# Operand sums of the FFN output placed between the products of the FFN input, in a ring of their own

## The chip, the cores and the metric

The kernel runs on one core of a Trainium2 chip. The core has five engines with queues of their own: TensorE (PE) multiplies matrices, VectorE (DVE) and ScalarE (ACT) work element by element, GpSimd (POOL) does the same and cannot read PSUM, and SyncE (SP) issues DMA transfers. Each engine runs its instructions in the order of its queue and waits at the first one that is not ready. The metric is the device time of one execution in microseconds.

## What is computed

One layer of a hybrid decoder on 1024 tokens of width 1024, in float32: token mixing, cross attention and a gated FFN. The change touches the last part:

```python
def conv_glu(hn, w_ffn_in, conv_w, conv_b, w_ffn_out):
    S = hn.shape[1]
    a, gate = jnp.split(hn @ w_ffn_in, 2, axis=-1)
    a_pad = jnp.pad(a, ((0, 0), (CONV_W - 1, 0), (0, 0)))
    conv = conv_b + sum(a_pad[:, j:j + S] * conv_w[j] for j in range(CONV_W))
    return (jax.nn.gelu(conv) * gate) @ w_ffn_out
```

`w_ffn_in` is 1024 x 5632 and `w_ffn_out` 2816 x 1024.

## The kernel before

Every float32 operand of a product is split into a high and a low part, and one product of tiles is three matmuls: high by high, high by low, low by high (`mm3`, L280 to L283). The two FFN products also use Strassen's scheme in Winograd's form: seven products of half the size take the place of eight, at the price of sums of operands before and of results after.

**FFN input.** The 2816 columns are worked in FT = 22 steps f of 128 columns of `a` and 128 of `gate`. For each f, `Weights` loads two raw tiles of 512 KB (L162), A with the columns of `a` and B with those of `gate`; the ring of raw tiles has two slots (`NRAW`). Four jobs turn them into seven pages of split weights (ring of 12, `NWP`). Job A splits two pieces of the first tile. Job B makes three sums on GpSimd (L199, L200, L201) and splits two pieces. Job C makes one more sum on GpSimd (L207) and splits two. Job D splits the last piece. Splitting is a cast on ScalarE (L175) and a subtraction on VectorE (L178), in `parts`. The raw slots come free with the last L178 of jobs C and D. In a steady f, the calls of `W.pump` do jobs C and D for f + 1, then A and B for f + 2.

`ffn_in(f)` issues the seven products (`product`, 12 matmuls each) and combines the results on VectorE (`add`, L1421) with three temporaries `p1`, `u2`, `v5`. Then come the convolution and GELU (L1458 on ScalarE, L1459 and L1460 on VectorE, L1461 on ScalarE), the product with the gate (L1462 on VectorE), and the store of 128 rows of the result to `u_d` in DRAM (L1463).

**FFN output.** Its Winograd operands are sums of blocks, four for each pair of f on the side of `u_d` and four on the side of `w_ffn_out`. They are made during the FFN input by `fo_sums(side, m)` and kept in DRAM (`us_d`, `ws_d`). A call loads four tiles of 256 KB (L1502), does four sums on GpSimd (L1505) and four stores from GpSimd's queue (L1521). The call stands at the end of an f: for the weights (`"w"`) at odd f, for the activations (`"u"`) at even f. A sum of `u` needs two rows of blocks that were stored by two f before.

The temporaries `p1`, `u2`, `v5`, the four tiles of each call and the residual tiles `hr` of the FFN output share one ring of nine 2 KB slots per partition (`w2`, L1153).

**Who sets the order.** From f = 1 on no engine's order is written by hand. The program goes to a planner (`schedule_with_timeline_sim=True`), which walks a simulated timeline and gives each engine the earliest instruction of the program that is ready there. The order of the source is a priority, then, and an instruction can run well before its place in the source when its operands and its slot are there. On the chip each engine keeps the order that the planner wrote down.

Of the kernel before, what the change touches and what calls it, by code (L numbers as in the profile page):

```python
# [9 lines left out]
F32 = mybir.dt.float32  # L10
# [4 lines left out]
OP = mybir.AluOpType  # L15
# [3 lines left out]
P = 128  # L19
# [25 lines left out]
def hybrid_layer(ctx, tc, I, out):  # L45
    nc = tc.nc
    pe, act, dve, pool, sp = nc.tensor, nc.scalar, nc.vector, nc.gpsimd, nc.sync

    def open_pool(name, **kw):
        st = ExitStack()  # L50
        p = st.enter_context(tc.tile_pool(name=name, bufs=1, reuse_waits="tile", **kw))
        return st, p
# [8 lines left out]
    def nm(s):  # L61
        cnt[0] += 1
        return f"{s}_{cnt[0]}"
# [216 lines left out]
    def mm3(o, lh, ll, rh, rl, start, stop):  # L280
        pe.matmul(o, lhsT=lh, rhs=rh, start=start, stop=False)  # L281
        pe.matmul(o, lhsT=lh, rhs=rl, start=False, stop=False)  # L282
        pe.matmul(o, lhsT=ll, rhs=rh, start=False, stop=stop)  # L283
# [10 lines left out]
    def kq(shape, dt, name):  # L294
        return wpool.tile(shape, dt, name=nm(name), tag="kq", bufs=4)
# [630 lines left out]
    for s in range(-4, NB):  # L926
        h, i = b_units[max(s, 0)]
        m = s % NT
# [137 lines left out]
    for s in range(-2, NA + 3):  # L1066
# [21 lines left out]
        u = s - 2  # L1088
# [59 lines left out]
    pgp = ctx.enter_context(tc.tile_pool(name="pgp", bufs=1, reuse_waits="tile"))  # L1148

    def page(shape, dt, name):  # L1150
        return pgp.tile(shape, dt, name=nm(name), tag="pg", bufs=28)

    def w2(shape, dt, name):  # L1153
        return pgp.tile(shape, dt, name=nm(name), tag="w2", bufs=9)

    def page_s():
        return pgp.tile([P, 512], F32, name=nm("ws"), tag="ws", bufs=1)
# [97 lines left out]
    def xo_unit(c, t, mid=None):  # L1255
        pages = W.get(("xo", c), 8)
        half, u = divmod(t, 4)
        p = accp()
        for k in range(KT):
            oh, ol = ox[k // 4, (k % 4) // 2, half]  # L1260
            s = slice(u * P, (u + 1) * P)
            if k == 4 and mid:
                mid()
            mm3(p, oh[:, k % 2, s], ol[:, k % 2, s], pages[k][:, 0, :], pages[k][:, 1, :], k == 0, k == KT - 1)
        hs = h2[t][:, c * 512:(c + 1) * 512]
        dve.tensor_tensor(hs, p, hs, op=OP.add)
        if t == NT - 1:
            W.free(8)
        W.pump(1)

    def f_norm(t):
        rs = slice(t * P, (t + 1) * P)
        act.dma_start(h2_d[rs, :], h2[t])
        st = small("st", (P, 12), 6)
        ws = [w2([P, 512], F32, "hn") for _ in range(1 if t >= 4 else 2)]
        norm_rows(h2[t], ws[0].bitcast(BF), st[:, 0:1], st[:, 1:2])
        hn = []
        for g in range(2):
            hg = h2[t][:, g * 512:(g + 1) * 512]
            w = hg if t >= 4 else ws[g]  # L1280
            dve.scalar_tensor_tensor(w, hg, st[:, 1:2], gff[g], op0=OP.mult, op1=OP.mult)
            hn.append(w)
        hst[t] = hn
# [31 lines left out]
    def xb_finish(name):  # L1315

        if name == "T4":
            xb_new(name)
            for u in range(4):
                xb_put(name, u, t4s[u], "a", "d")  # L1320
            return
        XB[name] = [[], []]
        for v in range(2):
            f = tf[name][v]
            hh, ll = (page([P, 2, 512], F32R, name) for _ in range(2))
            act.copy(hh, f)
            dve.tensor_tensor(ll, f, hh.bitcast(F32), op=OP.subtract)
            XB[name][0].append(hh)
            XB[name][1].append(ll)
# [75 lines left out]
    def product(w, xb):  # L1405
        o = (PB[nprod[0]] if nprod[0] < len(PB) else (accp, trp, big)[nprod[0] % 3])()[:, 0:512]
        nprod[0] += 1
        for k in range(4):
            ks = slice(k * P, (k + 1) * P)
            hh, hl = (XB[xb][i][k // 2][:, k % 2, :] for i in range(2))  # L1410
            mm3(o, w[:, 0, ks], w[:, 1, ks], hh, hl, k == 0, k == 3)
        W.free(1)
        return o

    def ffn_in(f):

        def wt(n):
            return W.get(("fi", f), n + 1)[n]

        def add(o, x, y):  # L1420
            dve.tensor_tensor(o, x, y, op=OP.add)  # L1421
        a, g = kq([P, T], F32, "fa"), kq([P, T], F32, "fg")
        lo, hi = slice(0, 512), slice(512, 1024)
        p1 = w2([P, 512], F32, "p1")
        P1 = product(wt(0), "B11")
        act.copy(p1, P1)
        if f == 0:
            yield
            add(a[:, lo], product(wt(1), "B21"), p1)
            yield  # L1430
            P3 = product(wt(5), "B22")
            yield
        u2, v5 = (w2([P, 512], F32, n) for n in ("u2", "v5"))
        add(u2, product(wt(2), "T2"), p1)
        W.pump(1)
        if f:
            add(a[:, lo], product(wt(1), "B21"), p1)
            W.pump(1)
        add(v5, product(wt(3), "T1"), u2)
        W.pump(1)  # L1440
        P7 = product(wt(4), "T3")
        add(g[:, hi], P7, v5)
        add(u2, P7, u2)
        W.pump(1)
        if f:
            P3 = product(wt(5), "B22")
        if f == FT - 1:
            for n in range(FLD):
                fo_load(n)
        add(a[:, hi], P3, v5)  # L1450
        add(g[:, lo], product(wt(6), "T4"), u2)
        W.pump(1)
        if f == FT - 1:
            for n in range(2):
                fo_prep(n)
            nprep[0] = 2
        cv = kq([P, T], F32, "fc")
        act.activation(cv, a, AF.Identity, bias=cw[:, f, 3:4], scale=cw[:, f, 2:3])  # L1458
        dve.scalar_tensor_tensor(cv[:, 1:], a[:, :T - 1], cw[:, f, 1:2], cv[:, 1:], op0=OP.mult, op1=OP.add)  # L1459
        dve.scalar_tensor_tensor(cv[:, 2:], a[:, :T - 2], cw[:, f, 0:1], cv[:, 2:], op0=OP.mult, op1=OP.add)  # L1460
        act.activation(cv, cv, AF.Gelu_apprx_tanh)  # L1461
        dve.tensor_tensor(g, cv, g, op=OP.mult)  # L1462
        act.dma_start(u_d[f * P:(f + 1) * P, :], g)  # L1463
        if f % 2:
            fo_sums("w", f // 2)
        elif f:
            fo_sums("u", f // 2 - 1)
        if f == FT - 1:
            fo_sums("u", f // 2)

# [19 lines left out]
    def sum_at(d, j, m):  # L1492
        return d[(j * NM + m) * P:(j * NM + m + 1) * P, :]

    def fo_sums(side, m):

        src, d = (u_src, us_d) if side == "u" else (w_src, ws_d)
        x = {}
        for odd in range(2):
            for half in range(2):  # L1500
                x[odd, half] = w2([P, 512], F32, "fs")
                sp.dma_start(x[odd, half], src(m, odd, half))  # L1502

        def sub(o, p, q, op=OP.subtract):
            pool.tensor_tensor(o, p, q, op=op)  # L1505
        if side == "u":
            a11, a12, a21, a22 = x[0, 0], x[1, 0], x[0, 1], x[1, 1]
            sub(a22, a21, a22, OP.add)
            sub(a21, a11, a21)
            sub(a11, a22, a11)  # L1510
            sub(a12, a12, a11)
            made = (a22, a11, a21, a12)
        else:
            b11, b21, b12, b22 = x[0, 0], x[1, 0], x[0, 1], x[1, 1]
            sub(b11, b12, b11)
            sub(b12, b22, b12)
            sub(b22, b22, b11)
            sub(b21, b21, b22)
            made = (b11, b22, b12, b21)
        for j, y in enumerate(made):  # L1520
            pool.dma_start(sum_at(d, j, m), y)  # L1521

    FO_X = {"1": lambda m: u_src(m, 0, 0), "2": lambda m: u_src(m, 1, 0), "4": lambda m: u_src(m, 1, 1),
            "5": lambda m: sum_at(us_d, 0, m), "6": lambda m: sum_at(us_d, 1, m), "7": lambda m: sum_at(us_d, 2, m),
# [5 lines left out]
    def fo_load(n):  # L1530
        if n >= len(fo_steps):
            return
        i, m = fo_steps[n]
        fo_raw[n] = page([P, 2, 512], F32, "fo")
        sp.dma_start(fo_raw[n][:, 0, :], FO_X[i](m))
        sp.dma_start(fo_raw[n][:, 1, :], FO_Y[i](m))

    def fo_prep(n):

        if n >= len(fo_steps):  # L1540
            return
        raw = fo_raw.pop(n)
        hi, lo = wp(), wp()
        act.copy(hi, raw)  # L1544
        dve.tensor_tensor(lo, raw, hi.bitcast(F32), op=OP.subtract)  # L1545
        fo_pg[n] = (hi, lo)

    with tc.manual_schedule(engines={mybir.EngineType.PE}):
        for t in range(NT):
            xo_unit(1, t, (lambda: f_tr(t - 2)) if t >= 2 else None)  # L1550
            f_norm(t)
        first = ffn_in(0)
        next(first)
        f_tr(6)
        next(first)
        f_tr(7)
        next(first)
        for n in ("T1", "T2", "T3", "T4"):
            xb_finish(n)
        for _ in first:  # L1560
            pass
    for f in range(1, FT):
        for _ in ffn_in(f):
            pass
# [112 lines left out]
```

## Time and profile before

| | us |
|---|---|
| median of 3 runs | 1742.68 |
| lowest and highest run | 1738.83, 1744.15 |
| profiled execution | 1739.45 |
| its span, first to last instruction | 1737.7 |
| mean granted clock of TensorE, share of full speed | 0.969 |

The rows further down come from the profiled execution. Their times count from the start of its span.

### The profile page before, as it was taken

The page shows a single profiled execution, that of the slowest core. Times are in us where ns is not written, and L with a number is a line of the kernel's source. Part 1 is how long each engine was busy: PE and PEld are TensorE (multiplying, and loading weights), DVE is VectorE, ACT ScalarE, POOL GpSimd, SP SyncE. Part 2 cuts the span into 40 slices and gives each one's busy share as a digit, 9 for nine tenths or more (in the row PEclk, how much of TensorE's full clock was granted, in tenths as well). Part 3 has the DMA queues.
Part 4 walks back from the last instruction along what each step waited for, and adds up shares of the span by engine and source line. Part 5 has one row for each costly group of instructions (what it writes and reads, how often), then busy time and mean ns, then how long its engine had stood idle before and what let it go on. Part 6 is the DMA issues. An engine that isn't in the chain of part 4 may idle for free. (4 is left out here: it accounts for less than half of the span.)

```text
span 1737.7 us, 22708 instructions
## 1 busy us (share of the span) xinstructions
PE 1585.9 (91%) x7660; PEld 1292.1 (74%) x7660; DVE 1255.5 (72%) x2461; ACT 737.3 (42%) x1469; POOL 676.5 (39%) x862
## 2 busy tenths in 40 slices
PE   8999898778888999989999979989898888989998
PEld 7788676667777779878777857767676666768887
DVE  5746998999999895367452798777666677745564
ACT  6545577566664236135431343332322232343432
POOL 2647567455320230231010065556655555541111
PEclk9999999899989999999999989999999999999999
DMA  8221134222131211342030223544444454799611
GB/s 281 88 85 57 63 103 158 70 92 75 53 98 39 95 61 49 127 158 85 25 110 12 86 73 134 177 147 152 154 157 164 163 170 166 258 356 391 239 43 49
DMA packets 117796, 220.08 MB, mean 127 GB/s; under 512 B 18480, under 2 KB 38448, under 8 KB 117680
## 3 DMA queue, kind: packets, MB, share of 16 engines
q1 hardware_dynamic: 103744, 171.44, 29.8%
q0 software_dynamic: 8320, 27.27, 4.1%
q10 hardware_dynamic: 5616, 19.93, 3.0%
q8 instruction: 60, 0.98, 0.2%
q14 instruction: 56, 0.46, 0.1%
HBM read 160.92 MB, written 57.67 MB: 126 GB/s over the span
## 5 line engine op out<-in xcount | busy, mean ns | idle before, releaser
L178 DVE TENSOR_TENSOR wp<-raw,wp 128x512 fp32r<-128x512 f32 (+1 forms) x200 | 166.8, 846 | 125.0 <-ACT wp L175 116.8
L175 ACT CAST wp<-raw 128x512 fp32r<-128x512 f32 (+1 forms) x188 | 111.4, 615 | 233.4 <-POOL raw L201 123.1
L1545 DVE TENSOR_TENSOR wp<-fo,wp 128x1024 fp32r<-128x1024 f32 x77 | 102.2, 1345 | 83.0 <-ACT wp L1544 64.6
L1505 POOL TENSOR_TENSOR fs<-fs,fs 128x512 f32<-128x512 f32 x88 | 128.7, 1462 | 40.1 <-DMA fs<-u_d 28.9
L1544 ACT CAST wp<-fo 128x1024 fp32r<-128x1024 f32 x77 | 79.5, 1049 | 118.5 <-PE trp L283 43.5
L281 PE MATMUL acc<-wp,xh 128*128 128x512 f32 (+1 forms) x272 | 110.4, 408 | 9.8 <-ACT X L619 9.8
L177 POOL TENSOR_SCALAR wp<-raw 128x512 fp32r<-128x512 f32 (+1 forms) x64 | 46.4, 735 | 177.8 <-DVE rst L110 63.5
L282 PE MATMUL acc<-wp,xh 128*128 128x512 f32 (+1 forms) x272 | 109.2, 403 | 0.0
L283 PE MATMUL acc<-wp,xl 128*128 128x512 f32 (+1 forms) x272 | 109.0, 401 | 0.0
L199 POOL TENSOR_TENSOR ws<-raw 128x512 f32<-128x512 f32 x21 | 28.7, 1365 | 188.6 <-DMA raw<-in_w_ffn_in_dram 181.8
L655 ACT COPY pt<-trp 128x512 f32<-128x512 f32 (+3 forms) x144 | 65.7, 476 | 70.8 <-PE trp L664 70.2
L178 POOL TENSOR_TENSOR wp<-raw,wp 128x512 fp32r<-128x512 f32 x52 | 69.2, 1347 | 45.4 <-ACT wp L175 45.3
L1010 PEld LDWEIGHTS acc<-va_t,pt 128*128 128x128 f32 x576 | 74.0, 195 | 6.7 <-ACT pt L655 4.6
L1587 POOL TENSOR_TENSOR hr<-hr,r 128x512 f32<-128x512 f32 x16 | 27.6, 1750 | 131.5 <-DVE r L1603 75.0
L1010 PE MATMUL acc<-va_t,pt 128*128 128x65 f32 x576 | 76.7, 273 | 2.1 <-ACT pt L655 1.6
L1055 POOL DMA_DIRECT2D h_d<-xr x16 | 9.4, 586 | 167.3 <-DVE xr L1054 148.9
L993 ACT ACTIVATE ea<-ea,sta 128x128 f32<-128x128 f32 (+7 forms) x64 | 49.3, 777 | 50.0 <-DVE sta L992 46.7
L281 PEld LDWEIGHTS acc<-wp,xh 128*128 128x128 f32 x272 | 52.8, 194 | 23.4 <-ACT X L619 12.0
L538 DVE TENSOR_SCALAR_CACHE_REDUCE jk<-mb,cx 128x640 bf16<-128x640 uint16 (+1 forms) x64 | 68.7, 1073 | 0.7
L1461 ACT ACTIVATE fc<-fc 128x1024 f32<-128x1024 f32 x22 | 23.3, 1061 | 100.7 <-DVE fc L1460 100.7
L538 DVE TENSOR_SCALAR_CACHE_REDUCE jk<-mb,cand 128x640 bf16<-128x640 bf16 (+3 forms) x60 | 64.4, 1074 | 0.4
L282 PE MATMUL acc<-wp,wp 128*128 128x512 f32 x152 | 61.1, 402 | 3.0 <-DVE wp L178 2.6
(419 smaller groups left out, 5184.5 us busy)
## 6 DMA issues: line engine op xcount, KB each, us to landing
raw<-in_w_ffn_in_dram SPq DMA_DIRECT2D x44, 512.0 KB, 4.5
fs<-in_w_ffn_out_dram SPq DMA_DIRECT2D x44, 256.0 KB, 6.3
u_d<-fg ACTq DMA_DIRECT2D x22, 512.0 KB, 4.1
ws_d<-fs POOLq DMA_DIRECT2D x44, 256.0 KB, 2.3
fs<-u_d SPq DMA_DIRECT2D x44, 256.0 KB, 5.1
us_d<-fs POOLq DMA_DIRECT2D x44, 256.0 KB, 2.3
fo<-us_d SPq DMA_DIRECT2D x44, 256.0 KB, 5.4
fo<-ws_d SPq DMA_DIRECT2D x44, 256.0 KB, 5.4
```

Source lines behind the costliest of these rows:

```text
L175: act.copy(pg[:, 0, :n], src)
L178: (dve if el == "d" else pool).tensor_tensor(pg[:, 1, :n], src, pg[:, 0, :n].bitcast(F32), op=OP.subtract)
L281: pe.matmul(o, lhsT=lh, rhs=rh, start=start, stop=False)
L282: pe.matmul(o, lhsT=lh, rhs=rl, start=False, stop=False)
L283: pe.matmul(o, lhsT=ll, rhs=rh, start=False, stop=stop)
L538: dve.tensor_scalar(jk[:, :n], src, th[:, j:j + 1], None, op0=OP.is_ge, op1=OP.add, accum_out=cnt[:, j:j + 1])
L655: act.copy(dst, src)
L993: last["act"] = act.activation(e[:, :n], e[:, :n], AF.Exp, bias=st[:, 0, h:h + 1], scale=-1.0)
L1010: pe.matmul(acc[:, hh * 65:hh * 65 + 65], lhsT=pt, rhs=va_t[:, kt, :], start=kt == 0, stop=kt == i)
L1505: pool.tensor_tensor(o, p, q, op=op)
L1544: act.copy(hi, raw)
L1545: dve.tensor_tensor(lo, raw, hi.bitcast(F32), op=OP.subtract)
```

## The change

The sums get a ring of four slots of their own (`fs`), and the other users of the shared ring get five slots from f = 1 on. `fo_sums` still issues its loads at the end of an f, but returns its four sums, each with its store right behind it, as steps to be issued later. `sums_step()` issues one of them, at four places between the products of the next f; after the last f the rest is issued at once.

```diff
+    w2_st, w2p = open_pool("w2p")
+    w2_at = [w2p, 9]
+
     def w2(shape, dt, name):
-        return pgp.tile(shape, dt, name=nm(name), tag="w2", bufs=9)
+        return w2_at[0].tile(shape, dt, name=nm(name), tag="w2", bufs=w2_at[1])
+
+    def fs():
+        return w2_at[0].tile([P, 512], F32, name=nm("fs"), tag="fs", bufs=4)
@@ ffn_in
         if f:
             add(a[:, lo], product(wt(1), "B21"), p1)
             W.pump(1)
+        sums_step()
         add(v5, product(wt(3), "T1"), u2)
         W.pump(1)
+        sums_step()
         P7 = product(wt(4), "T3")
         add(g[:, hi], P7, v5)
         add(u2, P7, u2)
         W.pump(1)
+        sums_step()
         if f:
             P3 = product(wt(5), "B22")
...
         add(a[:, hi], P3, v5)
+        sums_step()
         add(g[:, lo], product(wt(6), "T4"), u2)
         W.pump(1)
...
         act.dma_start(u_d[f * P:(f + 1) * P, :], g)
+        sums_step(4)
         if f % 2:
-            fo_sums("w", f // 2)
+            owed_sums.extend(fo_sums("w", f // 2))
         elif f:
-            fo_sums("u", f // 2 - 1)
+            owed_sums.extend(fo_sums("u", f // 2 - 1))
         if f == FT - 1:
-            fo_sums("u", f // 2)
+            sums_step(4)
+            owed_sums.extend(fo_sums("u", f // 2))
+            sums_step(4)
@@ fo_sums
-                x[odd, half] = w2([P, 512], F32, "fs")
+                x[odd, half] = fs()
                 sp.dma_start(x[odd, half], src(m, odd, half))
-        def sub(o, p, q, op=OP.subtract):
+        def one(j, o, p, q, op=OP.subtract):
             pool.tensor_tensor(o, p, q, op=op)
+            pool.dma_start(sum_at(d, j, m), o)
...
         if side == "u":
+            return [lambda: one(0, x22, x21, x22, OP.add), lambda: one(2, x21, x11, x21),
+                    lambda: one(1, x11, x22, x11), lambda: one(3, x12, x12, x11)]
+        return [lambda: one(0, x11, x12, x11), lambda: one(2, x12, x22, x12),
+                lambda: one(1, x22, x22, x11), lambda: one(3, x21, x21, x22)]
-        for j, y in enumerate(made):
-            pool.dma_start(sum_at(d, j, m), y)
+    owed_sums = []
+
+    def sums_step(n=1):
+        for _ in range(n):
+            if owed_sums:
+                owed_sums.pop(0)()
@@ after ffn_in(0)
+    w2_st.close()
+    w2_at[:] = [ctx.enter_context(tc.tile_pool(name="w2q", bufs=1, reuse_waits="tile")), 5]
     for f in range(1, FT):
```

## Rows read from the trace of the kernel before

**Rows 1.** The page's first line.

```profile
span 1737.7 us, 22708 instructions
```

**Rows 2.** Busy time of each engine in a window: us, engines, clock, DMA share, GB/s.

```profile
1075.00:1467.00 392.00, 354.06 (x1456) 276.47 (x1454) 275.23 (x289) 111.70 (x170) 227.57 (x205) 0.98 0.47 160
```

**Rows 3.** Timeline of TensorE: start, duration, engine, line, operation, tiles.

```profile
1266.81 0.39 PE L283 MATMUL acc<-T,wp 128*128 128x512 f32 x1
...
1268.44 0.39 PE L281 MATMUL trp<-B,wp 128*128 128x512 f32 x1
```

**Rows 4.** View of the raw weight tile, 1080 to 1500 us: durations min/median/max, waits, landings.

```profile
L178 DVE TENSOR_TENSOR wp<-raw,wp x108: 674/683/1783, 1079.6 to 1492.8; 128x512 fp32r<-128x512 f32 x108
...
L199 POOL TENSOR_TENSOR ws<-raw x18: 1296/1305/1315, 1082.1 to 1476.6; 128x512 f32<-128x512 f32 x18
...
  POOL ws L199: 162.6, 17
...
DMA to landing us min/median/max: 3.3/4.8/6.9
```

**Rows 5.** Timeline of GpSimd in a cycle with sums of the weights.

```profile
1244.89 1.31 POOL L199 TENSOR_TENSOR ws<-raw 128x512 f32<-128x512 f32 x1 [9.46 <-DMA raw<-in_w_ffn_in_dram]
...
1248.40 1.28 POOL L1505 TENSOR_TENSOR fs<-fs,fs 128x512 f32<-128x512 f32 x1
1249.64 1.28 POOL L201 TENSOR_TENSOR raw<-ws,raw 128x512 f32<-128x512 f32 x1
...
1252.70 1.28 POOL L207 TENSOR_TENSOR raw<-raw 128x512 f32<-128x512 f32 x1
...
1256.96 1.09 POOL L1521 DMA_DIRECT2D ws_d<-fs  x2
```

**Rows 6.** Timeline of GpSimd in a cycle with sums of the activations.

```profile
1224.42 1.28 POOL L201 TENSOR_TENSOR raw<-ws,raw 128x512 f32<-128x512 f32 x1
1225.66 1.30 POOL L1505 TENSOR_TENSOR fs<-fs,fs 128x512 f32<-128x512 f32 x1
1226.91 1.76 POOL L207 TENSOR_TENSOR raw<-raw 128x512 f32<-128x512 f32 x1
```

**Rows 7.** Timeline of ScalarE in the cycle of rows 5.

```profile
1250.95 0.62 ACT L175 CAST wp<-raw 128x512 fp32r<-128x512 f32 x1 [5.08 <-POOL raw L201]
...
1258.22 1.06 ACT L1461 ACTIVATE fc<-fc 128x1024 f32<-128x1024 f32 x1 [3.58 <-DVE fc L1460]
```

**Rows 8.** Timeline of VectorE in the cycle of rows 5.

```profile
1238.42 0.68 DVE L178 TENSOR_TENSOR wp<-raw,wp 128x512 fp32r<-128x512 f32 x1
...
1251.61 1.11 DVE L178 TENSOR_TENSOR wp<-raw,wp 128x512 fp32r<-128x512 f32 x1 [4.33 <-ACT wp L175]
...
1253.25 2.53 DVE L178 TENSOR_TENSOR wp<-ws,wp 128x512 fp32r<-128x512 f32 x1
1255.70 2.42 DVE L1460 SCALAR_TENSOR_TENSOR fc<-fa,cw,fc 128x1022 f32<-128x1022 f32 x1
...
1261.06 0.68 DVE L178 TENSOR_TENSOR wp<-raw,wp 128x512 fp32r<-128x512 f32 x1
```

**Rows 9.** Timeline of SyncE's DMA issues in the cycle of rows 5.

```profile
1236.12 3.34 SPq L162 DMA_DIRECT2D raw<-in_w_ffn_in_dram  x2
1239.52 2.38 SPq L1502 DMA_DIRECT2D fs<-in_w_ffn_out_dram  x4
```

**Rows 10.** SyncE's waits, 1080 to 1500 us: total, times, longest.

```profile
SPq L1502 <- DMA u_d<-fg: 25.5, 10, 9.5
```

**Rows 11.** VectorE's groups by line and shape, 1080 to 1500 us: busy, mean ns.

```profile
L1460 DVE SCALAR_TENSOR_TENSOR fc<-fa,cw,fc 128x1022 f32<-128x1022 f32 x19 | 45.0, 2367 | 0.0
L178 DVE TENSOR_TENSOR wp<-ws,wp 128x512 fp32r<-128x512 f32 x18 | 36.4, 2024 | 0.0
```

**Rows 12.** View of the convolution's tile: durations min/median/max in ns.

```profile
L1462 DVE TENSOR_TENSOR fg<-fc,fg x22: 1224/1226/2451, 1060.8 to 1521.7; 128x1024 f32<-128x1024 f32 x22
```

**Rows 13.** The page's DMA issues: count, KB each, median us to landing.

```profile
ws_d<-fs POOLq DMA_DIRECT2D x44, 256.0 KB, 2.3
```

More of the change, by code (lines that the diff above doesn't have):

```diff
@@ L1500, in fo_sums @@
             for half in range(2):
-                x[odd, half] = w2([P, 512], F32, "fs")
+                x[odd, half] = fs()
                 sp.dma_start(x[odd, half], src(m, odd, half))
-        def sub(o, p, q, op=OP.subtract):
+        def one(j, o, p, q, op=OP.subtract):
             pool.tensor_tensor(o, p, q, op=op)
+            pool.dma_start(sum_at(d, j, m), o)
+        x11, x21 = x[0, 0], (x[0, 1] if side == "u" else x[1, 0])
+        x12, x22 = (x[1, 0] if side == "u" else x[0, 1]), x[1, 1]
         if side == "u":
[L1507 to L1519, printed above, removed]
-        for j, y in enumerate(made):
-            pool.dma_start(sum_at(d, j, m), y)
+            return [lambda: one(0, x22, x21, x22, OP.add), lambda: one(2, x21, x11, x21),
[7 more added lines that the diff above has]
+                owed_sums.pop(0)()
     FO_X = {"1": lambda m: u_src(m, 0, 0), "2": lambda m: u_src(m, 1, 0), "4": lambda m: u_src(m, 1, 1),
```

## The prediction

> **What bounds the kernel now.** I read the page first, for the span of 1737.7 us [rows 1]. Then the windows, to see where TensorE waits, since a change on GpSimd can only pay there. In the FFN input (1075 to 1467 us) TensorE is busy 354 of 392 us [rows 2]; a busy time is modelled, so I take the pace from two starts of one matmul stream instead: seven matmuls from 1266.81 to 1268.44, 0.233 us each [rows 3]. One f has seven products of twelve matmuls, 84 x 0.233 = 19.6 us. The view of the raw weight tile gives the real pace: L199, the first GpSimd sum on the weights of an f, starts 18 times between 1082.1 and 1476.6 us, (1476.6 - 1082.1) / 17 = 23.2 us apart [rows 4]. So 3.6 us of every f is not TensorE's, some 65 us over 18 f, and something of period 23.2 sets it.
>
> That something is a loop through the second raw weight tile. In an f of the weights' sums (call it a w cycle): VectorE's last L178 of the old tile runs at 1238.42 for 0.68 [rows 8], SyncE then issues the second of two raw loads (the pair of L162 ends at 1236.12 + 3.34 = 1239.46 [rows 9]), GpSimd has been waiting for it and starts L199 at 1244.89 [rows 5], L201 starts at 1249.64 and lasts 1.28 [rows 5], ScalarE casts at 1250.95 [rows 7], VectorE goes from 1251.61 without a gap through L178 and L1460 to 1258.12 [rows 8], ScalarE's GELU L1461 starts at 1258.22 [rows 7], and the last L178 of this tile runs at 1261.06 to 1261.74 [rows 8]: 22.6 us from release to release. TensorE is not in it. L199 waits 162.6 us in 17 times for raw data [rows 4], 9.6 us per f: GpSimd has time to spare, and its sums matter only where they sit inside this loop.
>
> **The change, part by part.** *Adds nothing to the work:* four sums of 1.3 us and four stores of 0.55 us per f stay (1.09 for two [rows 5]), with the same 44 + 44 loads.
>
> *Sums moved in the program's order.* Before, the sums of f stand behind the GpSimd sums L199 to L201 of f + 2 and ahead of L207 of f + 2. After, they stand behind L207. In a w cycle the first sum runs between L199 and L201, from 1248.40 to 1249.64, 1.24 us on the loop [rows 5]; in the trace eight cycles have this order. The second stands ahead of L207, but VectorE reaches L207's result only behind L1460, which starts at 1255.70 [rows 8], while L207 ends at 1253.98 [rows 5]: off the loop. In the other cycles (u) the first sum starts at 1225.66, when L201 is done, and only L207 is delayed [rows 6]; nothing on the loop. Removed: 8 x 1.24 = 9.9 us. This holds if the planner, which put a sum into the hole ahead of L201, no longer does so; the sums have a lower place in its list now and L207 fills part of the hole. Bounds: 0 and 9.9; I take 9.9.
>
> *Sums beside VectorE.* VectorE's operations on two SBUF operands stretch when GpSimd computes: L178 on ws takes 2.53 in this cycle [rows 8] and 2.02 in the mean, L1460 2.37 in the mean [rows 11], against 0.68 for the L178 at 1238.42 and 1261.06, which have no sum beside them [rows 8]. The trace does not show what share the sums cause and what share L207 does. In the w cycle the row at 1253.25 spans the end of L207 and a sum. A bound for a gain: if all of L178's excess on ws (1.34) and half of L1460's 2.37 went, 2.5 us x 18 = 45 us. A bound for a loss is the second rival. Since the sums, already loaded, will start as soon as L207 ends, they stay beside the same operations, nearer to the row as it is than to either end; I take a gain of 0.2 us per f, 4 us, for one sum fewer ahead of L1460.
>
> The Trainium skill's page "SBUF — State Buffer", section "Who interferes with whom", says that a VectorE instruction with two SBUF inputs and a GpSimd instruction that reads SBUF exclude each other, and that the later one waits for the whole of the other. The 2.53 us row fits a wait through the end of two GpSimd operations. By it, spacing the sums out would block one VectorE operation per sum rather than fewer, which speaks against the change; the second rival prices that from rows.
>
> *Loads one f ahead.* In before the loads already run ahead: SyncE issues them right behind the raw loads (1239.52 [rows 9]) and the sums follow 9 us later. The loads of u wait at SyncE for the store of u_d, 25.5 us in 10 times [rows 10]; no ring lets them go earlier. The w loads could. Worth: raw loads land 3.3 to 6.9 us after issue, median 4.8 [rows 4]; the second one here took from about 1239.4 to 1244.9, 5.5, with 1 MB of sums' operands behind it on the same queue. If that were out of its way: up to 2.2 us per f, 40 us; if the operands go in front of it, a loss (the third rival). I take 0.
>
> *Rings.* Three FFN temporaries per f in 5 slots, and 16 residual tiles late, replace 9 shared slots; the operands get 4. The new ring takes over memory of the old one once, at f = 1, behind temporaries that the same adds have read by then. Of SyncE's waits on the operands' loads the largest is for the store of u_d [rows 10], and none is named for a store of the sums, which is what a ring would wait for. Bounds: 0 and the third rival; I take 0.
>
> Sum: 9.9 + 4 = 14 us. The profiled execution took 1739.45 us (span 1737.7 [rows 1]); 1739.5 - 14 = 1725.5. The median of the runs is 3.2 us above that execution, so on its scale 1729.
>
> **The rivals.**
> *Nothing moves on the loop (1737 to 1748).* The order on each queue is the planner's, not the source's: it already put the loads a cycle early and sums into holes. If it refills the hole ahead of L201, only the 4 us and noise remain.
>
> *The sums land on VectorE's last steps (slower).* If the sums spread into the stretch in which GpSimd waits for raw data, they meet L1462 and the last L178, both on the loop. L1462 takes 1.23 in the median and 2.45 at most [rows 12]; L178 on a raw tile 0.68 and 1.78 at most [rows 4]. Price 1.2 + 1.1 = 2.3 us per f, 41 us in 18, less the 14 gained: 1770. It decides when more than the 14 / 18 = 0.8 us per f comes back in this way. For it: that stretch is GpSimd's only idle one, and the new places in the program lie in it. Against it: sums whose operands are there start when L207 ends, and four of them with their stores are over by 1258, as now [rows 5].
>
> *SyncE's queue waits for the small ring (slower).* All four operands must be summed and stored before the next four loads. The last two stores are issued from 1256.96 to 1258.05 [rows 5] and land 2.3 us later [rows 13], at 1260.4; the second raw load is due at the release of 1261.74 [rows 8]. If the planner puts the operands' loads ahead of that load, four issues of 0.6 (2.38 / 4 [rows 9]) from 1260.4 hold it to 1262.8, 1.1 us; 1 MB then lies in front of it, and a raw load that took 5.5 us may take 6.9, the longest [rows 4]. 1.1 to 2.5 us in each of 18 f is 20 to 45, less the 14: 1749 to 1774. It decides when the last store lands after the second raw tile's release, 1.3 us later than now. For it: rings of exactly one set. Against it: u's loads wait for a store that is issued behind the release in any case, so a planner that knows this puts them behind.
>
> *The loop falls out altogether (1675 to 1712).* If sums leave VectorE's way and the operands leave the raw load's way, the loop (22.6 - 1.2 - 2.5 - 2.2 = 16.7) is below TensorE's 19.6, and up to 3.6 x 18 = 65 us come back: 1678 at the end, half of it at 1710.
>
> **How the numbers follow.** Small gain as summed, 1714 to 1737: 0.40. Loop falls out: 0.20. Nothing: 0.17. The two slower ones: 0.12 and 0.11. The likeliest gives 1729. The range leaves out the far half of the large gain and the far half of the slower cases: 1694 to 1760. No change is within 0.3%, 5.2 us of 1742.7, about what three runs that spread over 5.3 us can tell: same 0.17, faster 0.60, slower 0.23.
>
> **What would show it.** Right: on GpSimd L199, L200, L201, L207 in a row and then the sums; L199's starts 22.3 to 22.7 us apart instead of 23.2; L1460 still about 2.4; the wait of L199 for raw data shorter by about 0.6 us per f. Wrong, fast: L1460 near 1.3 and L199's starts 20 to 21 us apart. Wrong, slow: sums queued ahead of L199 so that its wait is for GpSimd or none, L1462 at 2.4 in the mean, or SyncE's L1502 waiting on stores of us_d and ws_d with L162 behind it. The FFN output should keep its time; if it moves by more than 5 us, the ring of 5 slots for the residual tiles is the cause that I costed at nothing.

## The result and the profile after

The changed kernel took 1755.58 us (median of 4 runs, 1754.25 to 1757.62) against 1741.16 for the kernel before on the same chip: ratio 1.0083, 95% interval 1.0062 to 1.0103. It is slower by 14 us, and 1729 was forecast. The profiled execution took 1757.62 us; the page's first line answers to [rows 1]:

```profile
span 1755.8 us, 22643 instructions
```

Where the 18.1 us between the spans lie is read from starts of the same instructions. L199 starts 18 times in the loop of the FFN input: from 1082.1 to 1476.6 us before, from 1083.5 to 1486.4 after, so 23.20 us apart before and 23.70 after. The start gives 1.4 us, the 17 intervals 8.4. From the last L199 to the first matmul of the FFN output ("the tail" below) it is 36.1 us before, 42.0 after: 5.9. The FFN output takes 220.4 and 223.4: 3.0. (What is left, -0.6, lies behind the last matmul.)

The view of the raw weight tile, 1080 to 1515 us of the changed kernel, answers to [rows 4]:

```profile
L178 DVE TENSOR_TENSOR wp<-raw,wp x108: 674/683/4766, 1080.3 to 1502.7; 128x512 fp32r<-128x512 f32 x108
...
L199 POOL TENSOR_TENSOR ws<-raw x18: 1297/1304/1753, 1083.5 to 1486.4; 128x512 f32<-128x512 f32 x18
...
  POOL ws L199: 108.7, 14
...
DMA to landing us min/median/max: 3.4/5.3/7.1
```

The median L178 is the old one; the longest has grown from 1783 to 4766 ns. It is the first L178 behind L201, and it takes about 4.7 us in 13 of 17 f (in none before). One such f on GpSimd, against [rows 5, 6] (L1518 are the sums, L1519 their stores):

```profile
1273.04 1.30 POOL L1518 TENSOR_TENSOR fs<-fs,fs 128x512 f32<-128x512 f32 x1
1274.30 2.27 POOL L201 TENSOR_TENSOR raw<-ws,raw 128x512 f32<-128x512 f32 x1
1276.52 0.56 POOL L1519 DMA_DIRECT2D us_d<-fs  x1
1277.10 1.30 POOL L1518 TENSOR_TENSOR fs<-fs,fs 128x512 f32<-128x512 f32 x1
1278.35 1.27 POOL L207 TENSOR_TENSOR raw<-raw 128x512 f32<-128x512 f32 x1
1279.55 0.56 POOL L1519 DMA_DIRECT2D us_d<-fs  x1
1280.13 1.27 POOL L1518 TENSOR_TENSOR fs<-fs,fs 128x512 f32<-128x512 f32 x1
...
1286.28 1.37 POOL L1518 TENSOR_TENSOR fs<-fs,fs 128x512 f32<-128x512 f32 x1 [1.86 <-DMA fs<-in_w_ffn_out_dram]
```

and on VectorE in the same f, against [rows 8]:

```profile
1277.27 4.70 DVE L178 TENSOR_TENSOR wp<-raw,wp 128x512 fp32r<-128x512 f32 x1 [1.84 <-ACT wp L175]
...
1282.49 1.64 DVE L178 TENSOR_TENSOR wp<-ws,wp 128x512 fp32r<-128x512 f32 x1
1284.05 1.27 DVE L1470 SCALAR_TENSOR_TENSOR fc<-fa,cw,fc 128x1022 f32<-128x1022 f32 x1
...
1286.50 2.24 DVE L1472 TENSOR_TENSOR fg<-fc,fg 128x1024 f32<-128x1024 f32 x1
```

Three things are to be seen. A sum still stands ahead of L201 (1273.04): the planner filled the hole again, in 14 of the 18 f, where it was 8 before. L178 starts 0.17 us into the next sum and ends at 1281.97, through that sum, L207, a store and another sum. And a sum of the next group, ready early, meets L1472 (2.24 in place of 1.2 us; so in 4 of 17 f).

VectorE's groups by line, 1075 to 1515 us, against [rows 11]: the steps that come behind the long L178 got shorter, as they find GpSimd's sums done.

```profile
L178 DVE TENSOR_TENSOR wp<-raw,wp 128x512 fp32r<-128x512 f32 x110 | 141.5, 1299 | 79.3 <-ACT wp L175 79.3
...
L1470 DVE SCALAR_TENSOR_TENSOR fc<-fa,cw,fc 128x1022 f32<-128x1022 f32 x20 | 30.6, 1528 | 0.0
...
L178 DVE TENSOR_TENSOR wp<-ws,wp 128x512 fp32r<-128x512 f32 x18 | 22.8, 1269 | 0.0
```

The tail is seen on SyncE's queue (timeline of the changed kernel; L1515 loads sums' operands, L1547 and L1548 the FFN output's):

```profile
1494.43 10.77 SPq L1515 DMA_DIRECT2D fs<-u_d  x4
1515.08 0.81 SPq L1515 DMA_DIRECT2D fs<-in_w_ffn_out_dram  x2
1515.99 0.39 SPq L1547 DMA_DIRECT2D fo<-u_d  x1
```

Two groups of operand loads stand ahead of the FFN output's first load; with only four slots each waits for the sums and stores of the group before it. That load is issued at 1515.99, 29.6 us behind the last L199; before, it was at 1496.71, 20.1 behind. What hangs on it, on ScalarE, VectorE and TensorE (L1556 casts the FFN output's first operand):

```profile
1521.90 1.05 ACT L1556 CAST wp<-fo 128x1024 fp32r<-128x1024 f32 x1 [9.25 <-DMA fo<-in_w_ffn_out_dram]
```

```profile
1527.59 0.68 DVE L1427 TENSOR_TENSOR v<-acc,u 128x512 f32<-128x512 f32 x1
```

```profile
1528.42 0.77 PE L281 MATMUL acc<-wp 128*128 128x512 f32 x1 [4.15 <-DVE v L1427]
```

ScalarE waits 9.25 us for the load, adds of the last f stand behind the FFN output's first splits in VectorE's queue, and TensorE waits 4.15 us for one of them; before, it went on without a gap. The last f's 84 matmuls ahead of it take 21.4 us at a granted clock of 0.92, against 19.7 us at 1.00 before. These two, 4.2 and 1.7, are the tail's 5.9 us.

### The profile page after: what moved, and what is told of

It is laid out like the page before. It is cut to its first block, busy times and chain, and to the rows that moved or that the text cites. A ratio compares the mean times of both kernels' runs of the same rounds, so it can differ in the third digit from the quotient of the medians.

```text
span 1755.8 us, 22643 instructions
## 1 busy us (share of the span) xinstructions
PE 1597.7 (91%) x7660; PEld 1303.6 (74%) x7660; DVE 1281.3 (73%) x2461; ACT 739.5 (42%) x1469; POOL 674.9 (38%) x862
## 4 chain that ended last, share of the span: by engine, by line
PE 40%; DVE 31%; DMA 11%; issue 9%; POOL 5%; ACT 3%; SPq 0%; POOLq 0%; DVEq 0%; ACTq 0%
PE acc L281 7%; PE acc L282 7%; PE acc L283 7%; DVE jk L538 5%; DVE wp L178 5%; DMA raw<-in_w_ffn_in_dram 5%; PE big L281 2%; PE big L283 2%; PE big L282 2%; PE big L1249 2%; POOL raw L201 2%; DVE fc L1470 2%; PE acc L1010 1%; DVE ea L992 1%; DVE e L747 1%
## 5 line engine op out<-in xcount | busy, mean ns | idle before, releaser
L178 DVE TENSOR_TENSOR wp<-raw,wp 128x512 fp32r<-128x512 f32 (+1 forms) x200 | 214.4, 1087 | 97.6 <-ACT wp L175 89.7
L1518 POOL TENSOR_TENSOR fs<-fs,fs 128x512 f32<-128x512 f32 x88 | 125.7, 1429 | 68.3 <-DMA fs<-in_w_ffn_out_dram 56.8
L1556 ACT CAST wp<-fo 128x1024 fp32r<-128x1024 f32 x77 | 79.7, 1049 | 128.3 <-PE big L283 47.3
L178 POOL TENSOR_TENSOR wp<-raw,wp 128x512 fp32r<-128x512 f32 x52 | 69.2, 1348 | 46.1 <-ACT wp L175 45.9
L199 POOL TENSOR_TENSOR ws<-raw 128x512 f32<-128x512 f32 x21 | 29.4, 1400 | 146.2 <-DMA raw<-in_w_ffn_in_dram 95.2
L1469 DVE SCALAR_TENSOR_TENSOR fc<-fa,cw,fc 128x1023 f32<-128x1023 f32 x22 | 42.6, 1937 | 27.5 <-ACT fc L1468 27.5
```

What stands on the lines that cost most here:

```text
L178: (dve if el == "d" else pool).tensor_tensor(pg[:, 1, :n], src, pg[:, 0, :n].bitcast(F32), op=OP.subtract)
```

## The experiments

The kernels ran on several chips, so they are compared by the ratio to the kernel before on the same chip; a time in us beside it is the median of that kernel's own runs. The columns behind the ratio are read from the traces. "Apart" is the mean distance of L199's 18 starts; "to L201", "first L178" and "to release" are means over 17 f of the time from L199's start to L201's end, of the first L178 behind it, and of the time from L199's start to the issue of the next second raw load, which VectorE's last L178 releases. All in us.

| kernel | ratio (95% interval) | apart | to L201 | first L178 | to release | tail | output |
|---|---|---|---|---|---|---|---|
| before | 1 | 23.20 | 4.86 | 1.12 | 17.2 | 36.1 | 220.4 |
| changed | 1.0083 (1.0062 to 1.0103) | 23.70 | 5.71 | 3.99 | 17.8 | 42.0 | 223.4 |
| 1 at once | 1.0114 (1.0101 to 1.0127) | 23.80 | 5.79 | 3.96 | 17.8 | 42.5 | 222.8 |
| 2 one ring | 1.0106 (1.0093 to 1.0119) | 24.28 | 4.77 | 2.81 | 18.5 | 40.5 | 219.1 |
| 3 behind L207 | 1.0164 (1.0151 to 1.0178) | 24.60 | 4.03 | 1.24 | 18.4 | 43.7 | 222.6 |
| 4 behind L207, one ring | 1.0043 (1.0030 to 1.0056) | 23.72 | 4.03 | 1.23 | 18.3 | 37.5 | 219.1 |
| 5 stores alone | 1.0110 (1.0087 to 1.0133) | 24.13 | 4.77 | 2.82 | 18.5 | 41.1 | 219.7 |
| 6 rings alone | 0.9993 (0.9980 to 1.0006) | 22.72 | 5.34 | 1.31 | 16.2 | 40.3 | 223.2 |
| 7 no sums | 0.9705 (0.9677 to 0.9732) | 20.50 | 4.05 | 1.24 | 15.2 | 35.2 | 220.6 |
| 8 gated | 0.9601 (0.9577 to 0.9626) | 19.50 | 4.37 | 1.21 | 13.6 | 42.7 | 209.6 |
| 9 stores grouped | 0.9979 (0.9970 to 0.9989) | 22.58 | 5.31 | 1.31 | 16.2 | 41.0 | 222.5 |
| 10 stores on SyncE | 0.9956 (0.9939 to 0.9974) | 22.73 | 4.04 | 1.17 | 17.3 | 42.3 | 219.6 |
| 11 gated, GpSimd's stores | 0.9681 (0.9663 to 0.9698) | 20.32 | 6.46 | 0.71 | 14.1 | 41.3 | 211.5 |
| 12 gated, small rings | 0.9626 (0.9608 to 0.9644) | 19.38 | 4.16 | 1.24 | 14.9 | 45.5 | 214.0 |

My first theory was that the planner's sum ahead of L201 holds the loop and the small rings hold the tail; the rival was that the delay itself, or SyncE's queue, costs the time. In what follows, theories A and B are those of each experiment's own expectation.

**1. Sums at once.** The change without its delay: rings and single stores stay.

```diff
             owed_sums.extend(fo_sums("u", f // 2 - 1))
+        sums_step(4)
```

> The changed kernel, but each group of four sums is issued at once behind its loads, where the kernel before issued them; the ring of four, the residual ring of five and each store right behind its sum stay. Theory A (the order that the ring and the stores give GpSimd's queue costs the time, the place in the program nothing): 1752 to 1759 us, L199 starts 23.6 to 23.8 us apart, the first L178 behind L201 mostly about 4.7 us, as in the changed kernel. Theory B (issuing the sums one f later is what costs): back towards the kernel before, 1740 to 1748 us, and starts of L199 about 23.2 us apart.

1763.1 us, some 4 us beyond what theory A gave, with the changed kernel's loop. The delay is not what costs: without it the kernel is no faster (5 us slower by the ratios, with intervals that just touch).

**2. One ring.** The change with its delay and single stores, but operands, temporaries and residual tiles from one ring of nine.

```diff
-        return w2_at[0].tile([P, 512], F32, name=nm("fs"), tag="fs", bufs=4)
+        return w2([P, 512], F32, "fs")
...
-    w2_at[:] = [ctx.enter_context(tc.tile_pool(name="w2q", bufs=1, reuse_waits="tile")), 5]
```

> The changed kernel with its delayed sums and the store behind each sum, but operands, p1, u and v and the residual tiles all from one ring of nine, as before. Theory A (the small rings cost the time): the tail from the last L199 to the first matmul of the FFN output goes back from 42 to about 36 us, the FFN output from 223 to 220 us, the loop to 23.2 to 23.4 us an f; 1738 to 1748 us in all. Theory B (the delay and the single stores cost it): 1752 us or more, with the loop at 23.7 us an f and the tail at 42 us.

1761.7 us: theory A missed. The FFN output went back (219.1) and the tail part of the way, but the loop grew to 24.28. The small rings do not make the loop slow here; without them it is longer.

**3 and 4. Sums behind L207**, with the two small rings and with one ring of nine. L207 is kept in `self.c207`:

```diff
-                owed_sums.pop(0)()
+                with tc.issue_after(W.c207.ins):
+                    owed_sums.pop(0)()
```

> The changed kernel with one thing added: every sum and its store stand behind L207 in GpSimd's queue, so that L199, L200, L201 and L207 follow one another and the four sums come behind them; the rings stay small. Theory A (the sum that was put ahead of L201 and the sums around L207 hold the loop): L199 to the end of L201 takes 4.0 us in every f, the first L178 behind it 1.1 to 1.8 us, the starts of L199 stand 22.0 to 22.9 us apart, and the time is 1728 to 1745 us with the tail still at 42 us. Theory B (the small ring holds SyncE's queue): now the operand loads stand between the two weight loads and wait for the late sums' stores; weight loads come late, starts of L199 stay at 23.7 us or above, 1755 to 1775 us.

> The same sums behind L207 in GpSimd's queue, with the one ring of nine instead of the two small rings. Theory A (order on GpSimd sets the loop, the small rings the tail and the FFN output): L199 to the end of L201 4.0 us, starts of L199 22.0 to 22.9 us apart, tail 36 us, FFN output 220 us: 1715 to 1735 us, faster than both kernels. Theory B (the sums cost VectorE the same wherever they run in an f): the loop stays at 23.2 us or more, 1737 to 1750 us.

1772.5 and 1751.5 us. The order on GpSimd is the one that I had forecast for the change, L199 to L201 takes 4.03 us in every f, and the loop is no shorter than before. What was saved ahead of L201 comes back behind it. (Each store still stands behind its sum here; kernel 10 shows the same without these stores.) VectorE's groups of kernel 4, 1080 to 1490 us (L1468 and L1469 are the two convolution steps):

```profile
L1469 DVE SCALAR_TENSOR_TENSOR fc<-fa,cw,fc 128x1022 f32<-128x1022 f32 x17 | 46.0, 2703 | 0.0
L1468 DVE SCALAR_TENSOR_TENSOR fc<-fa,cw,fc 128x1023 f32<-128x1023 f32 x17 | 44.0, 2590 | 2.4 <-ACT fc L1467 2.4
L178 DVE TENSOR_TENSOR wp<-ws,wp 128x512 fp32r<-128x512 f32 x17 | 24.2, 1422 | 0.0
```

Against 1.27 us without a sum (kernel 8), the two convolution steps wait 1.4 and 1.3 us, and this L178 0.7 (0.68 alone). So theory A fell, in 4 too, where the rings were out of the way, and the question became where a sum costs nothing. The time of 3 is the one that its theory B gave, and the rings cost 21 us between these two: in the loop (0.9 us an f, most of it between the second raw load's issue and L199, 6.1 against 5.5 us), the tail (6.2) and the output (3.5).

**5. Stores alone.** The kernel before, each store directly behind its sum; its sums at once, its ring of nine.

```diff
-        def sub(o, p, q, op=OP.subtract):
+        def sub(j, o, p, q, op=OP.subtract):
             pool.tensor_tensor(o, p, q, op=op)
+            pool.dma_start(sum_at(d, j, m), o)
...
-        for j, y in enumerate(made):
-            pool.dma_start(sum_at(d, j, m), y)
```

> The kernel before with one thing changed: each sum's store is issued right behind it; the sums stay where they were, in the one ring of nine. Theory A (a store directly behind L201 lets GpSimd's next sum start just ahead of VectorE's first L178, which then waits through several GpSimd instructions): the first L178 takes 4.7 us in every second f, the starts of L199 stand about 24.2 us apart as with the one ring and the delay, 1753 to 1763 us. Theory B (the delay by one f is what cost 18 us there): no change, starts of L199 23.2 us apart, 1740 to 1747 us.

1761.6 us: this one edit makes a loss as large as the change's, and with it the kernel takes as long as kernel 2, from which it differs by the delay only. Its trace has the long L178 in every second f; GpSimd and VectorE in one of them:

```profile
1255.66 0.56 POOL L1506 DMA_DIRECT2D ws_d<-fs  x1
1256.24 1.29 POOL L1505 TENSOR_TENSOR fs<-fs,fs 128x512 f32<-128x512 f32 x1
1257.48 1.27 POOL L207 TENSOR_TENSOR raw<-raw 128x512 f32<-128x512 f32 x1
1258.69 0.56 POOL L1506 DMA_DIRECT2D ws_d<-fs  x1
1259.27 1.27 POOL L1505 TENSOR_TENSOR fs<-fs,fs 128x512 f32<-128x512 f32 x1
```

```profile
1256.40 4.70 DVE L178 TENSOR_TENSOR wp<-raw,wp 128x512 fp32r<-128x512 f32 x1 [4.34 <-ACT wp L175]
```

**6. Rings alone.** The kernel before with the two rings of the change; sums at once, stores grouped.

```diff
-                x[odd, half] = w2([P, 512], F32, "fs")
+                x[odd, half] = fs()
...
+    w2_at[:] = [ctx.enter_context(tc.tile_pool(name="w2q", bufs=1, reuse_waits="tile")), 5]
```

> The kernel before with one thing changed: the two rings of the change (four for the operands, five for the others) in place of the one of nine; the sums at once, their stores grouped as before. Theory A (the small rings cost the tail and the FFN output by themselves): tail 40 to 42 us in place of 36, FFN output 222 to 223 us in place of 220, loop 23.2 to 23.6 us an f, 1749 to 1759 us. Theory B (the rings matter only together with the delay): 1741 to 1746 us.

1741.2 us, no change, but not for theory B's reason: tail and output grow by 4.2 and 2.8 us as theory A said, and a loop 0.48 us shorter (8.2 in 17 f) pays for it. A sum stands ahead of L201 in 9 of the 18 f, where it was 8. These f release the raw tile 16.9 us after L199, as such f did before. In the others, 8 of 17, the first of the four sums has already run ahead of L199, while GpSimd waited for raw data; three are left, and the release comes after 15.4 us, where f without a sum ahead of L201 took 17.4 before. That is where the loop got shorter.

**7. No sums.** Kernel 4 without the sums' arithmetic: operands are loaded and stored unsummed.

```diff
-            pool.tensor_tensor(o, p, q, op=op)
             pool.dma_start(sum_at(d, j, m), o)
```

> The sums behind L207 with the one ring of nine, but the sums' arithmetic is left out: the operands are loaded and stored unsummed, so the output is another. Theory A (the four sums hold the loop wherever they run between L199 and VectorE's last L178, by making VectorE's SBUF steps wait): the conv steps go back to 1.28 us and each L178 to 0.7 us, some 2.7 to 4.1 us less an f, starts of L199 19.6 to 21 us apart, 1675 to 1705 us. Theory B (the weight loads and the splits hold the loop by themselves): starts of L199 stay at 23 us or more, 1735 us or more.

1691.4 us, as theory A gave. The convolution steps take 1.28 us. Between L199 and the last L178 the four sums cost 23.72 - 20.50 = 3.2 us an f.

**8. Gated.** The delayed sums stand behind a one-column copy of the tile that VectorE's L1472 writes; SyncE issues the stores; one ring of nine. The single steps between the products go.

```diff
-        sums_step(4)
+        if owed_sums:
+            gate = pool.tensor_scalar(small("gate", (P, 1), 1), g[:, 1023:1024], 1.0, 1.0, op0=OP.mult, op1=OP.mult)
+            with tc.issue_after(gate.ins):
+                sums_step(4)
...
-            pool.dma_start(sum_at(d, j, m), o)
+            sp.dma_start(sum_at(d, j, m), o)
```

> The delayed sums all stand behind a one-column GpSimd copy of the gate tile that VectorE writes in L1472, so that they run when the conv and the splits of this f are over, in the 9 us in which GpSimd was idle; their stores are issued by SyncE, which has no work then; one ring of nine. Theory A (sums cost only what they meet between L199 and the last L178): VectorE's conv steps 1.28 us each, four sums of 1.3 us end ahead of the next L199, starts of L199 20 to 22 us apart, 1685 to 1720 us, faster than both. Theory B (the price moves along: the sums now hold back the next L199 or VectorE's L178 of the next A page): starts of L199 23 us apart or more, 1738 us or more.

1672.45 us, better than theory A's range. GpSimd in one f (L1470 is the gate, L1516 the four sums):

```profile
1221.76 1.30 POOL L207 TENSOR_TENSOR raw<-raw 128x512 f32<-128x512 f32 x1
1230.30 0.56 POOL L1470 TENSOR_SCALAR gate<-fg 128x1 f32<-128x1 f32 x1 [7.24 <-DVE fg L1467]
1230.83 5.75 POOL L1516 TENSOR_TENSOR fs<-fs,fs 128x512 f32<-128x512 f32 x4
1236.54 1.31 POOL L199 TENSOR_TENSOR ws<-raw 128x512 f32<-128x512 f32 x1
```

VectorE in the same f (L1464 and L1465 are the convolution steps):

```profile
1222.37 1.23 DVE L178 TENSOR_TENSOR wp<-raw,wp 128x512 fp32r<-128x512 f32 x1 [0.63 <-ACT wp L175]
1223.53 0.68 DVE L178 TENSOR_TENSOR wp<-ws,wp 128x512 fp32r<-128x512 f32 x1
1224.13 1.27 DVE L1464 SCALAR_TENSOR_TENSOR fc<-fa,cw,fc 128x1023 f32<-128x1023 f32 x1
...
1226.52 1.27 DVE L1465 SCALAR_TENSOR_TENSOR fc<-fa,cw,fc 128x1022 f32<-128x1022 f32 x1
```

And the window from 1020 to 1400 us (length, busy time of TensorE, its weight loads, VectorE, ScalarE, GpSimd; clock, DMA share, GB/s), against [rows 2]:

```profile
1020.00:1400.00 380.00, 376.78 (x1607) 301.87 (x1607) 281.78 (x356) 137.07 (x210) 216.34 (x167) 1.00 0.52 172
```

The sums fill what was GpSimd's idle time, both convolution steps run bare, and TensorE is busy 377 of 380 us: the loop has fallen below it. Of the 70 us the loop makes 63 (17 x 3.70) and the FFN output 11; the tail is 7 longer.

**9. Stores grouped.** The changed kernel, its four stores behind the fourth sum.

```diff
             pool.tensor_tensor(o, p, q, op=op)
-            pool.dma_start(sum_at(d, j, m), o)
+            made[j] = o
+            if len(made) == 4:
+                for k in range(4):
+                    pool.dma_start(sum_at(d, k, m), made[k])
```

> The changed kernel with its two rings and its delay by one f, but the four stores of a group are issued together behind the fourth sum, as in the kernel before. Theory A (the store directly behind each sum is what costs): the first L178 behind L201 1.1 to 1.8 us in every f in place of 4.7, starts of L199 22.6 to 23.2 us apart, 1737 to 1746 us. Theory B (the delay together with the small rings costs it): 1752 us or more, starts of L199 at 23.7 us.

1738.9 us: undoing the store's place undoes the loss and leaves 0.2% of gain. The planner does not keep the four stores together on the queue; what moves is the first of them. Span against the changed kernel: -19.1 us, of which L199's starts make 17 x 1.12 = 19.0. One f on GpSimd, then on VectorE:

```profile
1181.54 1.29 POOL L201 TENSOR_TENSOR raw<-ws,raw 128x512 f32<-128x512 f32 x1
1182.79 1.30 POOL L1520 TENSOR_TENSOR fs<-fs,fs 128x512 f32<-128x512 f32 x1
1184.03 0.56 POOL L1524 DMA_DIRECT2D us_d<-fs  x1
1184.61 1.30 POOL L207 TENSOR_TENSOR raw<-raw 128x512 f32<-128x512 f32 x1
...
1187.67 1.74 POOL L1520 TENSOR_TENSOR fs<-fs,fs 128x512 f32<-128x512 f32 x1
1189.36 1.09 POOL L1524 DMA_DIRECT2D us_d<-fs  x2
1196.82 1.78 POOL L1520 TENSOR_TENSOR fs<-fs,fs 128x512 f32<-128x512 f32 x1 [6.37 <-DMA fs<-in_w_ffn_out_dram]
```

```profile
1183.52 1.12 DVE L178 TENSOR_TENSOR wp<-raw,wp 128x512 fp32r<-128x512 f32 x1 [2.49 <-ACT wp L175]
1184.56 3.69 DVE L1470 SCALAR_TENSOR_TENSOR fc<-fa,cw,fc 128x1022 f32<-128x1022 f32 x1
...
1191.09 1.21 DVE L1472 TENSOR_TENSOR fg<-fc,fg 128x1024 f32<-128x1024 f32 x1
```

The first store stands one place later than in the changed kernel, and the sums end 12.7 us behind L199 (1189.41 - 1176.67), not 13.2 (1283.56 - 1270.33). L178 gets in after 1.12 us; L1470 then takes 3.69, but L1472 begins 14.4 us behind L199 and meets no sum, where it began at 16.2 us. The row at 1196.82 is the next group's first sum, in the stretch in which GpSimd waits for raw data.

**10. Stores on SyncE**, one ring of nine, no gate: only the second part of the diff of 8.

> The changed kernel with the one ring of nine and its delayed sums, their stores issued by SyncE; no gate. GpSimd's queue holds L199, L200, L201, then the four sums around or behind L207, back to back. Theory A (a sum costs wherever it meets VectorE's steps ahead of the last L178; the stores' place only shifts which step pays): starts of L199 22.6 to 23.8 us apart, 1735 to 1752 us, so that the gain of the gated kernel is the gate's. Theory B (the store's issue on GpSimd is the obstacle, and the gate adds nothing): 1670 to 1710 us.

1735.4 us, as theory A gave. Taking the stores off GpSimd without moving the sums brings 0.4%. No sum stands ahead of L201 here (4.04 us to L201), and the raw tile is released no earlier than before (17.3 us against 17.2). What the loop gains, 0.5 us, lies between the second raw load's issue and L199 (5.4 us against 5.95).

**11. Gated, with GpSimd's stores.** Kernel 8 without the second part of its diff.

> The gated kernel with one ring of nine, but GpSimd issues the stores itself, one behind each sum; in its queue the next L199 and L200 then stand between the last sums and stores. Theory A (the gate gives the gain): sums and stores take 8.7 us behind the gate, so L199 and L200 come some 0.5 to 2 us late, starts of L199 20.2 to 21.8 us apart, 1685 to 1720 us. Theory B (the gain needs the stores off GpSimd): 1730 us or more.

1686.8 us, theory A. The gate with the one ring, stores still on GpSimd, brings most of the gain; the stores on SyncE another 14 us, as sums and stores otherwise hold L200 and L201 (6.46 us to L201).

**12. Gated, with the change's two rings.**

> The gated kernel with its stores on SyncE and the two small rings of the change. Theory A (the small rings cost only the tail and the FFN output): starts of L199 19.9 to 20.2 us apart, some 0 to 9 us more than with one ring of nine: 1672 to 1683 us. Theory B (with so short a loop the ring of four holds SyncE's queue, where the operand loads wait for the stores and the weight loads behind them): starts of L199 20.6 us apart or more, 1685 us or more.

1677.8 us, theory A: 2.8 us more in the tail and 4.4 in the output than kernel 8, 0.12 less an f in the loop.

## Why the prediction was wrong

**The bound** was read rightly. The loop through the second raw tile, not TensorE, sets the pace: kernels 7, 8, 11 and 12 shorten it, and the loop stops at 19.4 to 19.5 us an f in 8 and 12, near the 19.6 that I had worked out for TensorE from [rows 3].

**The step that failed** is the first of the change: *Adds nothing to the work: four sums and four stores per f stay.* I took the store's new place, directly behind its sum, at nothing. The planner puts the first store directly behind L201, so that the next sum begins just ahead of VectorE's first L178 (1276.52 and 1277.10 above). With everything else held it costs, by the difference of the ratios times 1742 us, 19 us in the kernel before (5 against before), 21 with the small rings (1 against 6) and 18 with the delay as well (changed against 9). The traces show two effects of it: VectorE's first L178 takes 4.7 us rather than 1.1, and, in the changed kernel, the sums with their stores last longer and one reaches L1472. No run parts the two, but the f of the traces do so roughly. With four sums, one ahead of L201, the raw tile is released 16.8 us after L199 in kernel 9 and 18.7 in the changed kernel, where the first L178 is long; in the 5 f in which a fifth sum begins ahead of the release, and meets L1472 or the L178 ahead of it, 19.6. In kernel 5 the f with the long L178 release 1.5 to 3.0 us later than such f of the kernel before, and the f without it 0.5 later.

**The sums ahead of L201**, my 9.9 us of gain, failed twice over. The planner put more of them there (14 of the 18 f, not 0), which the first rival had foreseen. And the price was wrong: kernels 4 and 10 have none, save 0.8 us up to L201, and pay 1.9 and 0.9 us behind it (18.3 and 17.3 to release against 17.2). The trace of the kernel before could have told it. There the 7 f of 17 with such a sum release the raw tile 16.9 us after L199, and the 10 without after 17.4. The first convolution step, on VectorE, in an f with and in one without:

```profile
1245.90 1.38 DVE L1459 SCALAR_TENSOR_TENSOR fc<-fa,cw,fc 128x1023 f32<-128x1023 f32 x1 [1.38 <-ACT fc L1458]
```

```profile
1275.13 1.71 DVE L1459 SCALAR_TENSOR_TENSOR fc<-fa,cw,fc 128x1023 f32<-128x1023 f32 x1
```

With such a sum L1459 is done ahead of L201, while VectorE waits for it; in the others it comes behind L201 and lies on the loop. So I followed one kind of f around the loop and priced the sum there, without following the other kind. Whether the sum or the place of L1459 makes the difference was not tried.

**The sums beside VectorE**, 4 us of gain: the sign was wrong for the changed kernel. L1470 fell from 2.37 to 1.53 us and L178 on ws from 2.02 to 1.27 [rows 11], which my signs put beside a large gain, and the L178 ahead of them took more than both gave. The bound of 45 us was the better number: removing the sums wholly (7) or putting them behind L1472 (8) shortens the loop by 46 and 63 us in 17 f.

**The loads one f ahead** at nothing: right within what the runs tell with one ring (2 against 5: 0.7 us); with the small rings the delay brings 2 us (9 against 6) to 5 (changed against 1), by the ratios again, but in both pairs the intervals overlap.

**The rings** at nothing: right as a sum (6: 0.9993), wrong as a claim that nothing moves. Loop -8.2, tail +4.2, output +2.8 us. The output moved by 3.0 us in the changed kernel, under the 5 that I had named.

**The rivals.** *The sums land on VectorE's last steps* had the right side, and the row at 1286.50 is its mechanism, but it was to cost L1462 (now L1472) and the last L178; the greater weight lies on the first L178. *SyncE's queue* does not hold the loop of the changed kernel: the second raw load is issued 0.03 us after the last L178 of the old tile before, 0.02 after, and from there to L199 it is 5.95 us in the mean before and 5.82 after. It does hold the tail. *The loop falls out altogether* (1675 to 1712) is about what the gate brings (1672); the change itself put the sums nowhere near there.

## What to carry to other kernels

Two engines that shut each other out are ordered by which of their steps lie on the path. Count the stretch in which the other engine's steps are off it, and put the side work there with a dependency, since a planner may fill any hole it finds: here the one ahead of L201, in 8 and then in 14 of 18 f. A step that leaves a critical segment has not gained until the next segment is read too: here the 0.8 us saved ahead of L201 came back behind it. And where a loop has two kinds of turns, compare their lengths before one of them is priced. When issues are rearranged, price their new places in the queue, not only their number.

## What the runs showed of the hardware

The convolution step takes 1.27 us when GpSimd computes nothing and 2.6 to 2.7 us in the mean beside sums (kernels 8 and 4). A VectorE step mostly gets in at the end of the GpSimd instruction that it meets: 1.12 us at 1183.52, 1.23 at 1222.37. By the Trainium skill's page "SBUF — State Buffer", section "Who interferes with whom", whichever issues first holds the shared ports for its whole instruction and the other waits; those rows agree. The rows at 1277.27 and 1256.40 go beyond it: 4.70 us, through a sum, L207, the 0.56 us of a store and another sum, though three instructions had ended before L178 got in. There are 46 such L178 in the traces, of 4.67 to 4.78 us, all in the changed kernel and in kernels 1, 2 and 5, and each begins 0.15 to 0.17 us after a sum that follows a store. Why VectorE is passed over there, and not at 1183.52, stays open; it was not measured by itself.

The FFN output takes 209.6 us in kernel 8, 11 less than before, with the same 925 matmuls recorded. TensorE is busy for all of it at a granted clock of 1.00. Before and in the changed kernel it is idle for 8.6 and 8.1 us of the stage, and busy for 211.8 and 215.3 at a clock of 0.98 and 0.96. So most of the 11 us is idle time that is gone, and the rest goes with the clock; what took the idle time away was not looked into.
